# Factor tiles ahead of the activation tile, and branch outputs that start 4 to 52 bytes into longer buffers

## The chip, the cores and the metric

The kernel runs on one core of a Trainium2 chip. The metric is device time in microseconds (us); the time before is the median of two runs, 2579.45 us (2578.78 to 2580.13). Lower is better.

## The reference, cut to what matters

A two-layer decoder trunk on 256 tokens of width 2048, in float32. Each layer normalises `x`, makes one wide input projection, runs four branches on parts of it (A a state-space scan, B and D attention, C gated linear attention), projects each branch's output (width 1024) to 2048, weighs it with a sigmoid merge gate, sums the four, and applies one output projection:

```python
h = rmsnorm(x, pre_norm)
proj = h @ w_in                                   # 2048 x 20592
...                                               # out_a, out_b, out_c, out_d: (1, 256, 1024)
gates = jax.nn.sigmoid(merge.reshape(bsz, s, N_BRANCHES, D_MODEL))
mixed = (gates[:, :, 0] * (out_a @ w_branch[0]) + gates[:, :, 1] * (out_b @ w_branch[1])
         + gates[:, :, 2] * (out_c @ w_branch[2]) + gates[:, :, 3] * (out_d @ w_branch[3]))
return x + rmsnorm(mixed @ w_out, post_norm)
```

## The kernel before

All large products are computed on TensorE in the type `float32r`, each as three products of halves: an operand is split into a high half (its rounded copy) and a low half (the rest), and high x high, low x high and high x low are added up in PSUM. Two halves of everything therefore lie in SBUF:

- `hx`, in the pool `cp` (tiles that live as long as the kernel): the transposed activations of a layer, 16 blocks of 128 channels, in each block 256 tokens of the high half (`hh`) and 256 of the low half (`hl`).
- `hi` and `lo`, in the pool `st`, three buffers each: the halves of 1024 weight columns. `fetch` brings the raw weights from HBM into one of five `raw` buffers, ScalarE rounds them into `hi` (L165) and VectorE takes the difference into `lo` (L166).
- the tags `oh` and `ol` in `st`, one buffer each: the halves of whatever the next products read as activations: the normalised low-rank pair `cT`, then the branch outputs `oD`, `oC`, `oA`, `oB` one after the other, then the first half of the merged result (`m_h0`, `m_l0`). The second half of the merged result lies in slots of the pool `sl` (`m_h1`, `m_l1`). `transpose_split` fills them (L243 to L250).

A TensorE matmul has a *moving* operand, streamed from SBUF, and a *stationary* one, the weights, loaded ahead of it by a weight load (PEld in the profile). What is called weights by the model is not always what TensorE loads:

- `chunk_a` (L186 to L188) loads 128 x 128 pieces of the activations (`hx`, or the `oh`/`ol` tiles) and streams 512 columns of `hi` or `lo`. All merge gates (`acc_mA` to `acc_mD`), the branch projections (`acc_bA` to `acc_bD`), the output projection (`acc_y`) and most of the input projection go this way. One call with `hx` issues 96 matmuls (16 blocks, two token halves, three products), one call on a branch output 48.
- `chunk_b` (L203, L205, L207) loads pieces of `hi` and `lo` and streams `hx`: 512 columns (`hh` and `hl` together) with `hi`, then 256 columns (`hh`) with `lo`. `acc_g`, `acc_x`, `acc_f` go this way.
- `chunk_b4` (L228 to L230) loads pieces of `hi`/`lo` and streams 256 columns of `cT`. The `acc_small` product (L421 to L423) loads 112 columns of `hi`/`lo` and streams 256 of `hh` or `hl`.

A scheduler in the tile framework orders the instructions on each engine; the generators in `bg` (attention, scans, transposes) are stepped between weight tiles so that their small TensorE products fall between the large ones.

Tiles get their addresses in the order in which pools and tiles are made: a pool's tiles lie one behind the other, padded to 32 bytes, and a longer tile shifts all that come behind it. `cp` comes first (it ends with `hx`, `rt`, `rb`), then `st` (`raw`, `oh`, `ol`, `hi`, `lo`, `gt`), `sl` (the slots), `sm`. In each of the 128 partitions a tile starts at the same byte.

Of the kernel before, what the change touches and what calls it, by code (L numbers as in the profile page):

```python
# [9 lines left out]
F32 = mybir.dt.float32  # L10
F32R = mybir.dt.float32r
# [7 lines left out]
P = 128  # L19
T = 256  # L20
# [17 lines left out]
def trunk(ctx: ExitStack, tc: tile.TileContext, x, pos, vecs, rows, dskip, post, glaw2,  # L38
# [4 lines left out]
    cp = ctx.enter_context(tc.tile_pool(name="cp", bufs=1))  # L43
    st = ctx.enter_context(tc.tile_pool(name="st", bufs=1))
# [4 lines left out]
    def slot(i, name, dt=F32):  # L49
        return sl.tile([P, 2048], dt, tag=f"s{i}", name=name)  # L50

    def psT(name, shape=(P, 512)):
        return ps.tile(list(shape), F32, tag="t", name=name, bufs=2)
# [104 lines left out]
    def fetch(src, n=1024, own=None):  # L158
        if first_raw:
            raw = first_raw.pop(0)  # L160
        else:
            raw = st.tile([P, 1024], F32, tag="raw", name="raw", bufs=5)
            nc.sync.dma_start(raw[:, :n], src)
        hi, lo = own or (st.tile([P, 1024], F32R, tag=t, name=t, bufs=3) for t in ("hi", "lo"))
        S.copy(hi[:, :n], raw[:, :n])  # L165
        V.tensor_tensor(lo[:, :n], raw[:, :n], hi[:, :n].bitcast(F32), ALU.subtract)  # L166
        return hi, lo
# [52 lines left out]
    def chunk_b4(src, p0, nb, xh, xl, k0, name):  # L220
# [10 lines left out]
            step()  # L231
        return acc

    def transpose_split(src, nb, dh, dl, d0, scale, name):

        for b2 in range(nb // 2):
            pt = psT(f"tr_{name}{b2}").rearrange("p (a t) -> p a t", a=2)
            for j in range(2):
                for tt in range(2):
                    PE.transpose(pt[:, j, tt * P:(tt + 1) * P], src(tt, 2 * b2 + j), ident)  # L240
            d = slice(d0 + 2 * b2, d0 + 2 * b2 + 2)
            if scale is None:
                S.copy(dh[:, d], pt)  # L243
                V.tensor_tensor(dl[:, d], pt, dh[:, d].bitcast(F32), ALU.subtract)
            else:
                for j in range(2):
                    S.activation(dh[:, d0 + 2 * b2 + j], pt[:, j], AF.Copy, scale=scale(2 * b2 + j))
                for j in range(2):
                    b = 2 * b2 + j
                    V.scalar_tensor_tensor(dl[:, d0 + b], pt[:, j], scale(b), dh[:, d0 + b].bitcast(F32),  # L250
                                           ALU.mult, ALU.subtract)
            yield

    hx = cp.tile([P, 16, 2, T], F32R, tag="hx", name="hx")
    hh, hl = hx[:, :, 0], hx[:, :, 1]

    def sumsq(src, junk, acc):
        S.activation(junk, src, AF.Square, accum_out=acc)

    rt3 = cp.tile([P, 16], F32, tag="rt", name="rt")  # L260
    rt, rt2 = rt3[:, 0:2], rt3[:, 2:4]
    rb = cp.tile([P, T], F32, tag="rb", name="rb")

    def rb3(p_, n):
        return rb[p_].rearrange("p (o t) -> p o t", o=1).to_broadcast([p_.stop - p_.start, n, T])
# [120 lines left out]
    for l in range(DEPTH):  # L386
# [9 lines left out]
        cc = slot(5, "cc").rearrange("p (a b t) -> p a b t", a=2, b=2)  # L396
        cssq = small([P, 4], "cssq")
        lgate = slot(3, "lgate").rearrange("p (a b) -> p a b", a=2)
        oh = st.tile([P, 8, T], F32R, tag="oh", name="cT_h")
        ol = st.tile([P, 8, T], F32R, tag="ol", name="cT_l")  # L400
        ropej = slot(4, "qr").rearrange("p (a t) -> p a t", a=8)
        for i in range(2):
            if l == 0 and i == 1:
# [12 lines left out]
        for kh in range(2):  # L416
            hi, lo = fetch(w_sm[l, kh], 896)
# [85 lines left out]
        def cnorm_gen(l=l, cssq=cssq, cc=cc, oh=oh, ol=ol):  # L503
            r = rstd(cssq, 512, 4, "cn")
            for i in range(2):
                for tt in range(2):
                    V.tensor_scalar(cc[:, i, tt], cc[:, i, tt], r[:, 2 * i + tt:2 * i + tt + 1], None, ALU.mult)
                yield
                o = V_Q if i == 0 else V_KV
                yield from transpose_split(lambda tt, b: cc[:, i, tt, b * P:(b + 1) * P], 4, oh, ol, 4 * i,  # L510
                                           lambda b: vec[:, l, o + b:o + b + 1], f"c{i}")
# [25 lines left out]
        def mla_gen(l=l, qr=qr, qn=qn, kn=kn, dv_=dv_, lgate=lgate, oh=oh, ol=ol):  # L537
            for o, t in ((0, cos), (4, sin)):
                V.tensor_tensor(qr[:, o:o + 4], qr[:, o:o + 4],
                                t.rearrange("p (o n) -> p o n", o=1).to_broadcast([P, 4, T]), ALU.mult)  # L540
            V.tensor_tensor(qr[:, 0:4], qr[:, 0:4], qr[:, 4:8], ALU.add)
            yield

            def terms(h):
                return [(qn[:, h], kn[:, h]), (qr[:, h // 2], kr2[:, h % 2])]

            yield from attention(4, 128, 192 ** -0.5, terms, None, dv_, lgate, "D")
            noh = st.tile([P, 8, T], F32R, tag="oh", name="oD_h")
            nol = st.tile([P, 8, T], F32R, tag="ol", name="oD_l")
            res["D"] = (noh, nol)  # L550
            yield from transpose_split(lambda tt, b: lgate[:, tt, b * P:(b + 1) * P], 8, noh, nol, 0, None, "oD")

        res = {}
        mg = mla_gen()
        bg.append(mg)

# [136 lines left out]

        def finish(br, src, scale):
            def gen():
                noh = st.tile([P, 8, T], F32R, tag="oh", name=f"o{br}_h")
                nol = st.tile([P, 8, T], F32R, tag="ol", name=f"o{br}_l")
                res[br] = (noh, nol)
                yield from transpose_split(lambda tt, b: src[:, tt, b * P:(b + 1) * P], 8, noh, nol, 0, scale,
                                           "o" + br)  # L700
            g = gen()
            bg.append(g)
            return g
# [148 lines left out]
        drain()  # L852


        mh0 = st.tile([P, 8, T], F32R, tag="oh", name="m_h0")
        ml0 = st.tile([P, 8, T], F32R, tag="ol", name="m_l0")
        mh1 = slot(5, "m_h1", F32R).rearrange("p (a t) -> p a t", a=8)
        ml1 = slot(6, "m_l1", F32R).rearrange("p (a t) -> p a t", a=8)
        for half, (a_, b_) in enumerate(((mh0, ml0), (mh1, ml1))):
# [144 lines left out]
```

## Time and profile before

| | |
|---|---|
| median of the runs | 2579.45 us |
| the profiled execution | 2578.76 us |
| its span (first to last instruction) | 2577.0 us |
| TensorE (PE) busy | 2553.0 us, 99% of the span, 12666 matmuls |
| weight loads (PEld) busy | 2146.9 us, 83%, beside the matmuls |
| VectorE (DVE), ScalarE (ACT) busy | 1571.0 us (61%), 1284.7 us (50%) |
| DMA | 179 GB/s mean, the weights' queue 54.8% of the 16 engines' time |
| granted TensorE clock | 0.999 |

Matmuls are pipelined: a row's duration (some 390 ns for 512 columns) overlaps the next one's. What a matmul costs is the distance from its start to the start of the next. The tiles `oD`, `oC`, `oA`, `oB` stand in rows as `oD_h` and so on; the view leaves out numbers in names, so `m_h` is `m_h0` and `m_h1`.

### The profile page before, as it was taken

What the parts mean: (1) busy time and instruction counts of PE and PEld (TensorE: products, weight loads), DVE (VectorE), ACT (ScalarE), POOL (GpSimd) and SP (SyncE); (2) the same over time, 40 slices, a digit from 0 to 9 for tenths busy, and PEclk for the clock granted to TensorE, in tenths of its full rate; (3) what the DMA queues carried; (4) which work ended last, traced back from release to release, by engine and by line L of the source; (5) the groups of instructions that cost most, each with busy time, mean ns of one, the idle gap of its engine ahead of it and who ended that gap; (6) DMA issues with size and microseconds to landing.
All of it is one profiled execution on the core that took longest, in us unless ns stands there. A gap on an engine that the chain in (4) does not pass through costs nothing.

```text
span 2577.0 us, 32741 instructions
## 1 busy us (share of the span) xinstructions
PE 2553.0 (99%) x12666; PEld 2146.9 (83%) x12666; DVE 1571.0 (61%) x1956; ACT 1284.7 (50%) x1705; POOL 79.6 (3%) x75
## 2 busy tenths in 40 slices
PE   8999999999999999999999999999999999999998
PEld 7888888888888888888878888888888888888887
DVE  6756854776666555555566667547765665565555
ACT  6555544555445445444465455445554444444443
POOL 0000000000002000000000000000000010000000
PEclk9999999999999999999999999999999999999999
DMA  7554555555555555665655445455555655556654
GB/s 237 183 161 147 164 168 185 186 180 165 194 181 181 171 172 171 204 188 180 211 178 180 149 161 165 164 191 182 178 170 192 191 172 171 172 172 204 190 179 154
DMA packets 126571, 460.30 MB, mean 179 GB/s; under 512 B 14640, under 2 KB 15152, under 8 KB 125648
## 3 DMA queue, kind: packets, MB, share of 16 engines
q1 hardware_dynamic: 126144, 458.12, 54.8%
q8 instruction: 99, 1.62, 0.3%
q14 instruction: 56, 0.46, 0.1%
q10 hardware_dynamic: 272, 0.10, 0.0%
HBM read 453.97 MB, written 4.19 MB: 178 GB/s over the span
## 4 chain that ended last, share of the span: by engine, by line
PE 98%; ACT 1%; DVE 1%; issue 0%; DMA 0%; POOL 0%; SPq 0%; DVEq 0%; POOLq 0%; ACTq 0%
PE acc_f L203 4%; PE acc_x L203 3%; PE acc_f L205 2%; PE acc_mC L187 2%; PE acc_mA L187 2%; PE acc_mD L187 2%; PE acc_mA L186 2%; PE acc_mC L186 2%; PE acc_mA L188 2%; PE acc_mB L187 2%; PE acc_mB L186 2%; PE acc_mD L186 2%; PE acc_mC L188 2%; PE acc_mD L188 2%; PE acc_mB L188 2%; PE acc_g L203 2%
## 5 line engine op out<-in xcount | busy, mean ns | idle before, releaser
L166 DVE TENSOR_TENSOR lo<-raw,hi 128x1024 fp32r<-128x1024 f32 x842 | 1049.1, 1248 | 773.4 <-ACT hi L165 771.4
L165 ACT CAST hi<-raw 128x1024 fp32r<-128x1024 f32 x842 | 882.2, 1050 | 1035.5 <-PE acc_mB L188 95.2
L203 PE MATMUL acc_f<-hx,hi 128*128 128x512 f32 x480 | 171.5, 397 | 0.0
L205 PE MATMUL acc_f<-hx,lo 128*128 128x256 f32 x512 | 139.9, 283 | 0.0
L203 PE MATMUL acc_x<-hx,hi 128*128 128x512 f32 x360 | 128.8, 397 | 0.0
L203 PEld LDWEIGHTS acc_f<-hx,hi 128*128 128x128 f32 x480 | 90.2, 188 | 20.3
L205 PE MATMUL acc_x<-hx,lo 128*128 128x256 f32 x384 | 105.2, 284 | 0.0
L187 PE MATMUL acc_mA<-lo,hx 128*128 128x512 f32 x256 | 103.7, 405 | 0.0
L187 PE MATMUL acc_mC<-lo,hx 128*128 128x512 f32 x256 | 103.4, 404 | 0.0
L187 PE MATMUL acc_mD<-lo,hx 128*128 128x512 f32 x256 | 102.9, 402 | 0.0
L186 PE MATMUL acc_mA<-hi,hx 128*128 128x512 f32 x256 | 102.1, 399 | 0.0
L187 PE MATMUL acc_mB<-lo,hx 128*128 128x512 f32 x256 | 101.0, 395 | 0.0
L188 PE MATMUL acc_mA<-hi,hx 128*128 128x512 f32 x256 | 100.8, 394 | 0.0
L186 PE MATMUL acc_mC<-hi,hx 128*128 128x512 f32 x256 | 100.7, 393 | 0.0
L186 PE MATMUL acc_mD<-hi,hx 128*128 128x512 f32 x256 | 100.5, 392 | 0.0
L186 PE MATMUL acc_mB<-hi,hx 128*128 128x512 f32 x256 | 100.4, 392 | 0.0
L188 PE MATMUL acc_mC<-hi,hx 128*128 128x512 f32 x256 | 100.4, 392 | 0.0
L188 PE MATMUL acc_mD<-hi,hx 128*128 128x512 f32 x256 | 100.1, 391 | 0.0
L188 PE MATMUL acc_mB<-hi,hx 128*128 128x512 f32 x256 | 99.7, 390 | 0.0
L205 PEld LDWEIGHTS acc_f<-hx,lo 128*128 128x128 f32 x512 | 96.2, 188 | 2.9
L188 PE MATMUL acc_y<-hi,m_l 128*128 128x512 f32 x232 | 91.5, 394 | 0.0
L187 PE MATMUL acc_y<-lo,m_h 128*128 128x512 f32 x232 | 90.5, 390 | 0.0
(428 smaller groups left out, 5716.8 us busy)
## 6 DMA issues: line engine op xcount, KB each, us to landing
raw<-in_w_in_dram SPq DMA_DIRECT2D x624, 512.0 KB, 3.5
raw<-in_w_br_dram SPq DMA_DIRECT2D x128, 512.0 KB, 3.5
raw<-in_w_out_dram SPq DMA_DIRECT2D x64, 512.0 KB, 3.5
raw<-in_w_ukv_dram SPq DMA_DIRECT2D x16, 512.0 KB, 4.3
raw<-in_w_uq_dram SPq DMA_DIRECT2D x12, 512.0 KB, 3.8
x<-in_x_dram SPq DMA_DIRECT2D x4, 512.0 KB, 7.8
xr<-in_x_dram SPq DMA_DIRECT2D x2, 1024.0 KB, 6.8
pn<-in_post_dram SPq DMA_DIRECT2D x2, 1024.0 KB, 6.0
```

Of the source, the lines that this page charges most:

```text
L165: S.copy(hi[:, :n], raw[:, :n])
L166: V.tensor_tensor(lo[:, :n], raw[:, :n], hi[:, :n].bitcast(F32), ALU.subtract)
L186: PE.matmul(a2[tt], xh[:, k0 + k, ts_], hi[:, c], start=(k == 0), stop=False)
L187: PE.matmul(a2[tt], xh[:, k0 + k, ts_], lo[:, c], start=False, stop=False)
L188: PE.matmul(a2[tt], xl[:, k0 + k, ts_], hi[:, c], start=False, stop=(k == nk - 1))
L203: PE.matmul(acc[:, b], hi[:, c], hx[:, k].rearrange("p a t -> p (a t)"), start=(k == 0), stop=False)
L205: PE.matmul(acc[:, b, 0:T], lo[:, c], hh[:, k], start=False, stop=False)
```

## The change

Three edits, all of them to addresses:

1. `rt` (64 bytes in a partition) and `rb` (1024 bytes) are made ahead of `hx` instead of behind it.
2. The buffers of the tags `oh` and `ol` get 16 more elements (64 bytes).
3. The branch outputs start some elements into these buffers, the same number in `oh` and `ol`: D 1 and 2 (layer 0 and 1), C 5 and 4, A 9 and 12, B 13 and 3 elements of 4 bytes. `cT` and the first half of the merged result start at 0.

```diff
+    def halves(name, o=0):
+
+        h, lo = (st.tile([P, 8 * T + 16], F32R, tag=t, name=f"{name}_{t[1]}") for t in ("oh", "ol"))
+        return [a[:, o:o + 8 * T].rearrange("p (a t) -> p a t", a=8) for a in (h, lo)]
...
+    rt3 = cp.tile([P, 16], F32, tag="rt", name="rt")
+    rt, rt2 = rt3[:, 0:2], rt3[:, 2:4]
+    rb = cp.tile([P, T], F32, tag="rb", name="rb")
     hx = cp.tile([P, 16, 2, T], F32R, tag="hx", name="hx")
     hh, hl = hx[:, :, 0], hx[:, :, 1]
...
-    rt3 = cp.tile([P, 16], F32, tag="rt", name="rt")
-    rt, rt2 = rt3[:, 0:2], rt3[:, 2:4]
-    rb = cp.tile([P, T], F32, tag="rb", name="rb")
...
-        oh = st.tile([P, 8, T], F32R, tag="oh", name="cT_h")
-        ol = st.tile([P, 8, T], F32R, tag="ol", name="cT_l")
+        oh, ol = halves("cT")
...
-            noh = st.tile([P, 8, T], F32R, tag="oh", name="oD_h")
-            nol = st.tile([P, 8, T], F32R, tag="ol", name="oD_l")
+            noh, nol = halves("oD", (1, 2)[l])
...
-                noh = st.tile([P, 8, T], F32R, tag="oh", name=f"o{br}_h")
-                nol = st.tile([P, 8, T], F32R, tag="ol", name=f"o{br}_l")
+                noh, nol = halves("o" + br, {"C": (5, 4), "A": (9, 12), "B": (13, 3)}[br][l])
...
-        mh0 = st.tile([P, 8, T], F32R, tag="oh", name="m_h0")
-        ml0 = st.tile([P, 8, T], F32R, tag="ol", name="m_l0")
+        mh0, ml0 = halves("m0")
```

No instruction is added, removed or moved: on all engines the rows of the two programs agree one by one but for line numbers and the new names of two tiles (`m0_h`, `m0_l`). What differs is where operands start. The table gives the start of a tile in its partition, in bytes, and its remainder by 256, since the pieces that matmuls read are 512, 1024 or 2048 bytes apart and so keep that remainder (`acc_small` alone steps through its weights by 448 bytes):

| tile | before | mod 256 | after | mod 256 |
|---|---|---|---|---|
| `hx` | 25344 | 0 | 26432 | 64 |
| `raw`, first of five | 59200 | 64 | 59200 | 64 |
| `oh` (`cT_h`, `m_h0`) | 79680 | 64 | 79680 | 64 |
| `oh`, branch outputs | 79680 | 64 | 79684 to 79732 | 68 to 116 |
| `ol` (`cT_l`, `m_l0`) | 87872 | 64 | 87936 | 128 |
| `ol`, branch outputs | 87872 | 64 | 87940 to 87988 | 132 to 180 |
| `hi` and `lo`, first of each | 96064, 108352 | 64 | 96192, 108480 | 192 |
| slots, among them `m_h1`, `m_l1` | 157504, 182080 | 64 | 157632, 182208 | 192 |

## The prediction

> **What bounds the kernel now.** I read the page first: its head, the busy shares, the clock, and the chain that ended last.
>
> ```profile
> span 2577.0 us, 32741 instructions
> ## 1 busy us (share of the span) xinstructions
> PE 2553.0 (99%) x12666; PEld 2146.9 (83%) x12666; DVE 1571.0 (61%) x1956; ACT 1284.7 (50%) x1705; POOL 79.6 (3%) x75
> ...
> PEclk9999999999999999999999999999999999999999
> ...
> ## 4 chain that ended last, share of the span: by engine, by line
> PE 98%; ACT 1%; DVE 1%; issue 0%; DMA 0%; POOL 0%; SPq 0%; DVEq 0%; POOLq 0%; ACTq 0%
> ```
>
> TensorE is busy for 99% of the span and makes 98% of the chain, at full granted clock throughout. Then the waits of TensorE, longest first:
>
> ```profile
> engine line waited for: us in total, times, longest us
> PE tr_x L347 <- DMA x<-in_x_dram: 5.3, 1, 5.3
> PE tr_x L347 <- DVE xtot L364: 1.7, 1, 1.7
> ```
>
> The longest is the first load of `x`, and the next is 1.7 us. So no other engine's time is on the path, and a change that only moves addresses can move the end in one way: through the distance from one matmul's start to the next. I read those from the timeline, in stretches without foreign work, taking a group's first row and the first row of the group behind it.
>
> ```profile
> 1152.86 0.39 PE L186 MATMUL acc_bB<-hi,oB_h 128*128 128x512 f32 x1
> ...
> 1163.74 0.39 PE L186 MATMUL acc_mB<-hi,hx 128*128 128x512 f32 x1
> ...
> 1185.71 0.39 PE L186 MATMUL acc_bB<-hi,oB_h 128*128 128x512 f32 x1
> ```
>
> One call of `chunk_a` on a branch output is 48 matmuls: 1163.74 - 1152.86 = 10.88 us, or **226.7 ns** each. One on `hx` is 96: 1185.71 - 1163.74 = 21.97 us, or **228.9 ns** each. Shape, type, engine and source of the streamed columns are the same in both, and nothing waits. What differs is where the loaded piece starts: `oB` at 64 modulo 256 like `hi` and `lo`, `hx` at 0. I call the loaded start minus the streamed one, modulo 256, the *distance*: 0 for the branch output, -64 for `hx`. A distance of 0 is 2.2 ns cheaper at 512 columns.
>
> `chunk_b` has the roles exchanged, so its distance is +64. Here is a stretch of 31 pairs (512 columns, then 256), and beside it a group of 96 matmuls of 256 columns at distance 0, `acc_uq`:
>
> ```profile
> 729.73 0.40 PE L203 MATMUL acc_f<-hx,hi 128*128 128x512 f32 x1
> ...
> 740.67 0.40 PE L203 MATMUL acc_f<-hx,hi 128*128 128x512 f32 x1
> ...
> 113.06 0.28 PE L228 MATMUL acc_uq<-cT_h,hi 128*128 128x256 f32 x1
> ...
> 124.58 0.28 PE L228 MATMUL acc_ur<-cT_h,hi 128*128 128x256 f32 x1
> ```
>
> A pair takes (740.67 - 729.73) / 31 = **352.9 ns**, and a 256-column matmul at distance 0 takes 11.52 / 96 = **120.0 ns**. A pair at distance 0 would be 226.7 + 120.0 = 346.7 ns, so a distance of +64 costs 6.2 ns a pair. Both comparisons say the same: TensorE's pace depends on how the two operands lie to each other.
>
> **The change part by part.** No instruction comes, goes or moves, and every queue has its old order, so the sum has distances alone. By the table of addresses:
>
> - `hx` with `hi`/`lo`: `chunk_a` goes from -64 to -128, `chunk_b` from +64 to +128. In both, modulo 256, this is half a period; modulo 128 it is 0.
> - branch outputs in `chunk_a`: from 0 to -128 (high half) and -64 (low half), plus 4 to 52 bytes.
> - `cT` and the first half of the merged result: from 0 to 128 and 64 (sign by role). The second half keeps 0.
>
> The trace of before shows 0, -64 and +64 for full-sized matmuls, and so not 128, nor any distance that is no multiple of 64. Each price is therefore a choice between bounds.
>
> *hx, 5760 matmuls in `chunk_a`* (30 calls of 96 a layer, two layers). If the pattern repeats every 128 bytes, 128 is as good as 0 and they gain 2.2 ns each: -12.6 us. If it repeats every 256, the nearest rows are the two neighbours, -64 (2.2 ns over the best) and +64 (up to 6.2 over it if the whole of a pair's excess sits on one matmul): 0 to +4.0 ns each, 0 to +23 us.
>
> *hx, 1152 pairs in `chunk_b`*. The count is the 256-column rows of `acc_f`, `acc_x`, `acc_g`:
>
> ```profile
> L205 PE MATMUL acc_f<-hx,lo 128*128 128x256 f32 x512 | 139.9, 283 | 0.0
> ...
> L205 PE MATMUL acc_x<-hx,lo 128*128 128x256 f32 x384 | 105.2, 284 | 0.0
> ...
> L205 PE MATMUL acc_g<-hx,lo 128*128 128x256 f32 x256 | 70.6, 286 | 0.0
> ```
>
> With a period of 128 they gain 6.2 ns each: -7.1 us. With 256 they stay about where they are.
>
> *Branch outputs, 1536 matmuls* (four branches, two layers, four calls of 48). They are at the best distance now. A start that is 4 to 52 bytes off is shown nowhere. At worst each pays the whole excess of a pair, 6.2 ns: +9.5 us. At best the odd start frees a matmul of the part that does not scale with its columns: 226.7 - 120.0 = 106.7 ns is the price of 256 columns, which leaves 120.0 - 106.7 = 13.3 ns; without that, -20 us. I take the price of the nearest row, 2.2 ns: +3.4 us.
>
> *`cT` and the first merged half*, 576 and 384 matmuls, at the same 2.2 ns: +1.3 and +0.8 us, because their low halves land 64 off.
>
> The stores into the odd starts cost nothing that counts:
>
> ```profile
> L243 ACT CAST oB_h<-tr_oB x8: 575/586/594, 1063.3 to 2350.7; 128x512 fp32r<-128x512 f32 x8
> L244 DVE TENSOR_TENSOR oB_l<-tr_oB,oB_h x8: 678/680/684, 1064.7 to 2352.1; 128x512 fp32r<-128x512 f32 x8
> ```
>
> The 0.6 and 0.7 us stores of `oB` run beside the first merge call of B, which reads `hx` and lasts 22 us, and twice their time would still fit. Without that cover, doubled stores would cost 4 x 1.3 us a branch and layer. The split of the weights is covered too:
>
> ```profile
> L166 DVE TENSOR_TENSOR lo<-raw,hi 128x1024 fp32r<-128x1024 f32 x842 | 1049.1, 1248 | 773.4 <-ACT hi L165 771.4
> L165 ACT CAST hi<-raw 128x1024 fp32r<-128x1024 f32 x842 | 882.2, 1050 | 1035.5 <-PE acc_mB L188 95.2
> ```
>
> `raw` against `hi` goes from distance 0 to 128 there. A weight tile feeds 12 matmuls of 229 ns, 2.7 us, against 1.25 us of VectorE and 1.05 of ScalarE, which idle 773 and 1036 us before these lines, so even a tenth more would be hidden.
>
> The sum for a period of 128: -12.6 - 7.1 + 3.4 + 1.3 + 0.8 = -14.2 us, against the profiled execution's 2578.8 us: 2564.6 us. That execution is 0.7 us under the median, so I say **2565**. The bounds of the odd starts alone spread it from 2541 (all fixed parts gone) to 2571; I hold the lower end for remote.
>
> [...] A branch output's weight load lasts 188 ns and lies beside a matmul of 227:
>
> ```profile
> L186 PEld LDWEIGHTS acc_bB<-hi,oB_h x128: 187/188/188, 1086.0 to 2475.9; 128*128 128x128 f32 x128
> ```
>
> [...]
>
> **The rivals.**
>
> *The period is 256 (slower).* Then `hx` and the branch outputs all sit half a period off. [...] For it speaks the pace of `acc_small`, the only group whose distance passes through 0 and 128 (weights in steps of 448 bytes). At 0, then at 128:
>
> ```profile
> L421 PE MATMUL acc_small<-hx,hi 128*112 128x256 f32 x1 | 0.3, 276 | 0.0
> ...
> L421 PE MATMUL acc_small<-hx,hi 128*112 128x256 f32 x1 | 0.3, 282 | 0.0
> ```
>
> The matmul at 128 lasts 6 ns longer. Against it: these loads have 112 columns, every step also changes the next one's distance, and 128-column loads at distance 0 (`acc_uq`) last 283 ns, as long as the one at 128 here, so the order of prices is another one at this size. The price: `hx` half-way, 2.0 x 5760 = +11.5 us; 2496 matmuls on `oh`/`ol` half-way between 2.2 and 6.2 over the best, 4.2 x 2496 = +10.5; together +22, **2601 us**. With the upper bounds throughout, +23 and 6.2 x 2496 = +15.5, it is 2617. It decides from the point where 128 costs `hx` more than 1.2 ns over 0: then (2.2 - 1.2) x 5760 = 5.8 us of gain no longer outweigh the 5.5 us of the branch, `cT` and merged terms.
>
> *Nothing moves.* The 2.2 ns may belong to how `hh` and `hl` are interleaved, 1024 bytes apart, and not to the start: all `hx` matmuls have both. Then the first edit does nothing, and the rest gives 0 to +6 us: **2579 to 2584 us**. Then `acc_f` says against it that `hx` as the streamed operand has a loss too, where `hl` is only the second half of one stream. [...] That the change does not do what it says is excluded by the table of addresses.
>
> **How the numbers follow.** Chances: period of 128, 0.45 (2554 to 2574); nothing, 0.20 (2575 to 2584); period of 256, 0.33 (2584 to 2617); odd starts that free the fixed part, 0.02. The forecast's own range is 2556 to 2573. The range that holds 8 in 10 is 2555 to 2606: below lie about 0.04, and above it the upper third of the slower case, 0.12. A change of 2%, about what a measurement of this kernel can tell from none, would be 2528 or 2631. No case reaches either with its likely price: faster 0.02, same 0.95, slower 0.03.
>
> **What would show it.** In the profile after, `chunk_a` calls on `hx` at 21.77 us per 96 matmuls (226.7 ns) and pairs of `acc_f` at 347 ns would show the period of 128; calls at 22.1 us or more (230 ns) would show 256; 21.97 again, the interleaving. Branch calls stand at 10.88 us now: 10.99 is my price, 11.2 the upper bound, under 10.8 a gain from odd starts. The waits of TensorE should stay at 5.3 and 1.7 us. I am wrong if the time leaves the sum of these groups, that is if VectorE or ScalarE rows (1248 and 1050 ns for a weight tile) grow so far that TensorE begins to wait for `hi` or `lo`.

## The result and the profile after

The changed kernel takes 2604.82 us (two runs, 2604.12 and 2605.51) against 2579.45: a ratio of 1.010 (95% interval 1.008 to 1.012, as in the brackets below). It is slower by 25 us, where the forecast was 14 us faster. In size this is under the 2% that the forecast counted as a change; its direction is the rival's, "the period is 256", which gave 2601.

The head of the page after, its busy shares, the clock and the shares of the chain that ended last:

```profile
span 2603.7 us, 32741 instructions
PE 2580.4 (99%) x12666; PEld 2152.6 (83%) x12666; DVE 1571.9 (60%) x1956; ACT 1283.7 (49%) x1705; POOL 79.7 (3%) x75
...
PEclk9999999999999999999999999999999999999999
...
PE 98%; ACT 1%; DVE 1%; issue 0%; DMA 0%; POOL 0%; SPq 0%; DVEq 0%; POOLq 0%; ACTq 0%
```

The instructions, the clock and the chain are what they were; PE busy grew by 27.4 us and the span by 26.7. TensorE's longest waits are short as before:

```profile
PE tr_x L352 <- DMA x<-in_x_dram: 6.4, 2, 4.6
PE acc_c L186 <- ACT hi L165: 2.0, 1, 2.0
```

So the time is again in the spacing of matmuls. The timeline of the changed kernel, the first row of a branch call in layer 0, of the merge call behind it, and of the branch call after that; then the same three places in layer 1:

```profile
1130.30 0.40 PE L186 MATMUL acc_bB<-hi,oB_h 128*128 128x512 f32 x1
...
1141.60 0.39 PE L186 MATMUL acc_mB<-hi,hx 128*128 128x512 f32 x1
...
1164.00 0.40 PE L186 MATMUL acc_bB<-hi,oB_h 128*128 128x512 f32 x1
...
2424.86 0.40 PE L186 MATMUL acc_bB<-hi,oB_h 128*128 128x512 f32 x1
...
2435.85 0.39 PE L186 MATMUL acc_mB<-hi,hx 128*128 128x512 f32 x1
...
2458.16 0.39 PE L186 MATMUL acc_bB<-hi,oB_h 128*128 128x512 f32 x1
```

A call on `hx` takes 22.40 and 22.31 us, **233.3** and **232.4 ns** a matmul, against 228.9 before. That is over the 22.1 us that the prediction named as the sign of 256. The calls on `oB` take 11.30 us (235.4 ns, 13 elements in) and 10.99 us (229.0 ns, 3 elements in), against 10.88 before. The pairs of `acc_f`, 31 of them as before:

```profile
736.52 0.39 PE L203 MATMUL acc_f<-hx,hi 128*128 128x512 f32 x1
...
747.38 0.40 PE L203 MATMUL acc_f<-hx,hi 128*128 128x512 f32 x1
```

They take 350.3 ns, 2.6 less than before. The split of the weights stays covered:

```profile
L166 DVE TENSOR_TENSOR lo<-raw,hi 128x1024 fp32r<-128x1024 f32 x842 | 1049.5, 1248 | 793.0 <-ACT hi L165 789.0
L165 ACT CAST hi<-raw 128x1024 fp32r<-128x1024 f32 x842 | 880.9, 1048 | 1061.8 <-PE acc_mB L188 97.7
```

1248 ns as before and 1048 against 1050, with longer idle times ahead of them: the added time is not theirs.

From all starts in the two timelines (gaps that hold another product left out), mean ns by group, and what they make of the time:

| group | before | after | count | us |
|---|---|---|---|---|
| `chunk_a` on `hx` | 229.45 | 232.61 | 5760 | +18.2 |
| branch outputs | 227.5 | 232.4 | 1536 | +7.6 |
| merged result, first half | 227.4 | 233.0 | 384 | +2.1 |
| `cT`: 512 and 256 columns | 228.2, 120.0 | 233.2, 120.8 | 96, 480 | +0.9 |
| merged result, second half | 227.0 | 227.5 | 384 | +0.2 |
| `chunk_b` on `hx`, pairs | 352.7 | 350.7 | 1152 | -2.4 |

The sum is +26.6; the two profiled executions differ by 2605.51 - 2578.76 = 26.8 us. The second merged half, the one group that keeps distance 0, is the one that hardly moved. The pairs are at a distance of 128 now and gained a little.

### The profile page after: what moved, and what is told of

It reads as the page before. It is cut to its first block, busy times and chain, and to the rows that moved or that the text cites. A ratio compares the mean times of both kernels' runs of the same rounds, so it can differ in the third digit from the quotient of the medians.

```text
span 2603.7 us, 32741 instructions
## 1 busy us (share of the span) xinstructions
PE 2580.4 (99%) x12666; PEld 2152.6 (83%) x12666; DVE 1571.9 (60%) x1956; ACT 1283.7 (49%) x1705; POOL 79.7 (3%) x75
## 4 chain that ended last, share of the span: by engine, by line
PE 98%; ACT 1%; DVE 1%; issue 0%; DMA 0%; POOL 0%; SPq 0%; DVEq 0%; POOLq 0%; ACTq 0%
PE acc_f L203 4%; PE acc_x L203 3%; PE acc_mC L187 2%; PE acc_f L205 2%; PE acc_mA L187 2%; PE acc_mD L187 2%; PE acc_mA L188 2%; PE acc_mC L186 2%; PE acc_mB L187 2%; PE acc_mA L186 2%; PE acc_mB L188 2%; PE acc_mD L186 2%; PE acc_mB L186 2%; PE acc_mD L188 2%; PE acc_mC L188 2%; PE acc_y L188 2%
## 5 line engine op out<-in xcount | busy, mean ns | idle before, releaser
L166 DVE TENSOR_TENSOR lo<-raw,hi 128x1024 fp32r<-128x1024 f32 x842 | 1049.5, 1248 | 793.0 <-ACT hi L165 789.0
L165 ACT CAST hi<-raw 128x1024 fp32r<-128x1024 f32 x842 | 880.9, 1048 | 1061.8 <-PE acc_mB L188 97.7
```

## The experiments

### One half of the change at a time

Edit 1 alone (`rt` and `rb` ahead of `hx`, buffers and starts as before) puts everything at 64, that is at distance 0:

```diff
-        oh, ol = halves("cT")
+        oh = st.tile([P, 8, T], F32R, tag="oh", name="cT_h")
+        ol = st.tile([P, 8, T], F32R, tag="ol", name="cT_l")
```

and so for the branch outputs and the merged result.

> Edit 1 alone: the factor tiles ahead of hx, branch buffers as before. All operands of the large products then start at 64 modulo 256. Theory R (the price is set by the distance between the loaded and the streamed start, modulo 256): hx calls of chunk_a go from 228.9 to 226.7 ns a matmul, pairs of chunk_b from 352.9 to about 346.7 ns, branch calls stay at 226.7; 5760 x 2.2 + 1152 x 6.2 = 20 us less, 2559 us. Rival I (the interleaving of hh and hl makes hx dear, not its start): 2579 us, 228.9 ns as before. Rival M (the first edit itself is what costs): slower than 2579 us.

Measured: **2570.92 us**, ratio 0.997 [0.996, 0.998]. This part of the change is faster than before, by 7.8 us, where 20 were expected. Its timeline at the place shown above:

```profile
1115.79 0.39 PE L186 MATMUL acc_bB<-hi,oB_h 128*128 128x512 f32 x1
...
1126.67 0.39 PE L186 MATMUL acc_mB<-hi,hx 128*128 128x512 f32 x1
...
1148.43 0.39 PE L186 MATMUL acc_bB<-hi,oB_h 128*128 128x512 f32 x1
```

The call on `hx` now takes 21.76 us, 226.7 ns, like one on a branch output. So the 2.2 ns of before belonged to the start of `hx` and not to its interleaved halves, and "nothing moves" is refuted. The gain on `hx` is smaller than 2.2 x 5760 = 12.7 us because the stretches that small float32 products interrupt don't reach 226.7 at once. In the same kernel, the first matmul behind such a product, the ninth after it and the ninth after that:

```profile
836.73 0.39 PE L187 MATMUL acc_fv<-lo,hx 128*128 128x512 f32 x1
...
838.81 0.39 PE L187 MATMUL acc_fv<-lo,hx 128*128 128x512 f32 x1
...
840.85 0.39 PE L187 MATMUL acc_fv<-lo,hx 128*128 128x512 f32 x1
```

The first nine take 2.08 us (231 ns each), the next nine 2.04 (226.7). The kernel has 86 such stretches of twenty or more matmuls, and by the starts in the trace each is back at 226.7 within ten. Over all calls on `hx` the mean is 228.24, against 229.45 before: 7.0 us. The pairs were to give 7.1 and give 1.8 (351.2 ns against 352.7): at distance 0 they do not come down to the 346.7 that the prediction put together from two other groups, so most of its 6.2 ns was no matter of distance. The two gains make 8.8 us by these means, 1.0 more than the times differ.

Edits 2 and 3 alone leave `hx` at 0, while `hi` and `lo` go to 192, so its distance is +64:

```diff
-    rt3 = cp.tile([P, 16], F32, tag="rt", name="rt")
...
     hx = cp.tile([P, 16, 2, T], F32R, tag="hx", name="hx")
...
+    rt3 = cp.tile([P, 16], F32, tag="rt", name="rt")
```

> Edits 2 and 3 alone: hx stays at 0 modulo 256, hi and lo go to 192, branch outputs as in the change. Distance of hx in chunk_a becomes +64, in chunk_b -64. Theory R: branch calls at about 232.5 ns as in the change (1536 x 5.8 = +9 us), the first merged half and cT +3 us; hx at +64 is new: between the price of -64 (no change, so 2591 us in all) and that of 128 (+3.7 x 5760 = +21 us, 2612 us). Pairs of chunk_b at -64: 346 to 353 ns, 0 to -8 us. Rival O (the odd starts make the whole loss): 2604 us with hx calls at 228.9 ns.

Measured: **2608.3 us**, ratio 1.012 [1.010, 1.013].

```profile
1143.50 0.39 PE L186 MATMUL acc_mB<-hi,hx 128*128 128x512 f32 x1
...
1165.90 0.40 PE L186 MATMUL acc_bB<-hi,oB_h 128*128 128x512 f32 x1
```

A call on `hx` at +64 takes 22.40 us, 233.3 ns; at -64 it took 228.9. With a period of 128 these two distances would be one and the same. This row by itself excludes it for `chunk_a`.

### The change without the odd starts

```diff
-        return [a[:, o:o + 8 * T].rearrange("p (a t) -> p a t", a=8) for a in (h, lo)]
+        return [a[:, 0:8 * T].rearrange("p (a t) -> p a t", a=8) for a in (h, lo)]
```

> The change with all branch outputs at element 0 of the longer buffers. Theory R: hx and its distance of 128 are as in the change (232.6 ns), the branch calls sit at 128 (high half) and -64 (low half) without the odd bytes, which should be worth less than 2 ns a matmul: 1536 x 2 = 3 us, so 2602 to 2608 us. Rival O (the odd starts make the loss): back to 2579 us.

Measured: **2605.17 us**, ratio 1.010 [1.009, 1.012], as the change itself. All branch groups now have means of 232.6 to 233.1 ns, where the odd starts gave 228.9 to 235.5. So an offset of 4 to 52 bytes moves a branch by -4 to +3 ns and the eight of them cancel; what cost the branches their 5 ns is the 64 bytes that each buffer grew by (with the old buffers, in edit 1 alone, their groups have 226.7 to 228.2).

### Everything shifted by 128

Edit 1 with an unused tile of 128 bytes in front of all others, so that every remainder changes and no distance does:

```diff
+    cp.tile([P, 32], F32, tag="shift", name="shift")
```

> Edit 1 with an unused 128-byte tile ahead of everything: all starts move by 128, all distances stay 0. Theory R: as edit 1 alone, 2559 us, within 1 us. Rival A (what counts is a start's own remainder, with 64 as the good one): hx calls over 228 ns, 2579 us or more.

Measured: **2570.56 us**, ratio 0.997 [0.996, 0.998], the same as edit 1. At distance 0, then, moving both operands by 128 bytes changes nothing: how they lie to each other counts, not where they lie.

### hx alone at a distance of 128

Edit 1 with the 128 bytes of the tile `id2` made behind `hx` in place of ahead of it. The small tiles made between the two places move with `hx`; the branch outputs, `hi` and `lo` stay:

```diff
-    id2 = cp.tile([P, 32], F32R, tag="id2", name="id2")
     lvl = cp.tile([P, 8, P], U8, tag="lvl", name="lvl")
...
+    id2 = cp.tile([P, 32], F32R, tag="id2", name="id2")
```

> The first edit, and the identity tile id2 made behind hx in place of ahead of it, so that hx alone starts 128 bytes further and everything else keeps distance 0 or 128 (the pairs, hx against the activation's counterpart, too). The theory that the distance on hx carries most of the loss: 2570.9 + 5760 x (232.6 - 228.2 ns) = 2596, with hx calls of about 22.3 us. The rival that the branch outputs' starts and the merged product carry it: 2571, with hx calls of 21.8 us.

Measured: **2595.25 us**, ratio 1.006 [1.004, 1.008].

```profile
1127.33 0.40 PE L185 MATMUL acc_bB<-hi,oB_h 128*128 128x512 f32 x1
...
1138.27 0.40 PE L185 MATMUL acc_mB<-hi,hx 128*128 128x512 f32 x1
...
1160.58 0.40 PE L185 MATMUL acc_bB<-hi,oB_h 128*128 128x512 f32 x1
```

The calls on `hx` take 22.31 us (232.4 ns) and those on the branch outputs stay at 10.9. From edit 1, 128 bytes cost 24.3 us. The small products, which also read some of the moved tiles, take 176 us in both kernels, and the pairs of `chunk_b` 350.7 ns against 351.2, so the loss is in `chunk_a` on `hx`. Its mean is 232.6 ns, as in the change, against 229.45 before: that is about the +18.2 of the table, and the term that the forecast had at -12.6.

### Small distances

Everything at distance 0, and the branch outputs at offsets around it, in one buffer for both halves (D keeps its 1 and 2; `rt` has 8 columns, which gives the room):

```diff
-        h, lo = (st.tile([P, 8 * T + 16], F32R, tag=t, name=f"{name}_{t[1]}") for t in ("oh", "ol"))
+        both = st.tile([P, 16 * T + 64], F32R, tag="ohl", name=name)[:, o:o + 16 * T].rearrange("p (h a t) -> p h a t", h=2, a=8)
...
-                noh, nol = halves("o" + br, {"C": (5, 4), "A": (9, 12), "B": (13, 3)}[br][l])
+                noh, nol = halves("o" + br, {"C": (4, 8), "A": (12, 60), "B": (56, 63)}[br][l])
```

> Everything starts at the same remainder of 256 bytes (distance 0 for hx, the activation tile and the merged product), and the branch outputs start at o floats in one buffer for both halves: layer 0 / layer 1 at a distance of 4 / 8 bytes (D), 16 / 32 (C), 48 / 240 (A), 224 / 252 (B). The two small tiles and the buffers differ in size from the change, no work is left out. Theory G (starts count in steps of 64 bytes, so that anything within 64 bytes of distance 0 costs 226.7 ns): the branch groups stay at 226.7 and the time is that of the first edit alone, 2571. Theory E (only equal starts are cheap; any other distance costs the 229 to 235.5 ns that the change showed): branch groups at 229 to 235, time 2571 + 1536 x (2 to 9 ns) = 2574 to 2585. Theory C (a curve: the price rises with the distance): 4 and 252 bytes nearest to 226.7, 48 and 224 nearest to 232; about 2576.

Measured: **2575.95 us**, ratio 0.999 [0.998, 1.000]. The calls of D in layer 0 (+4 bytes) and of B in layer 0 (224) and layer 1 (252):

```profile
414.16 0.39 PE L186 MATMUL acc_bD<-hi,oD 128*128 128x512 f32 x1
...
425.32 0.40 PE L186 MATMUL acc_mD<-hi,hx 128*128 128x512 f32 x1
...
1117.40 0.39 PE L186 MATMUL acc_bB<-hi,oB 128*128 128x512 f32 x1
...
1128.59 0.39 PE L186 MATMUL acc_mB<-hi,hx 128*128 128x512 f32 x1
...
2396.05 0.39 PE L186 MATMUL acc_bB<-hi,oB 128*128 128x512 f32 x1
...
2406.93 0.39 PE L186 MATMUL acc_mB<-hi,hx 128*128 128x512 f32 x1
```

They take 11.16, 11.19 and 10.88 us: 232.5, 233.1 and 226.7 ns. Theory G falls, since 4 bytes cost as much as 128. C and E both have the time, but C falls as a curve: in uninterrupted stretches +4 takes 232.4, +8 230.7, +16 226.7, +32, +48 and 224 233.2, and 240 and 252 226.7. E lacks the cheap 16, 240 and 252. The next runs put one of these on all of `hx`.

### hx four bytes after and four bytes before

Edit 1 with a longer buffer for `hx`; o is 1, then 63:

```diff
-    hx = cp.tile([P, 16, 2, T], F32R, tag="hx", name="hx")
+    hx = cp.tile([P, 16 * 2 * T + 64], F32R, tag="hx", name="hx")[:, o:o + 32 * T].rearrange("p (k h t) -> p k h t", k=16, h=2)
```

> The first edit, with hx one float into a longer buffer: its distance to hi and lo is +4 bytes, all other large products stay at 0. The price seen on a branch output at +4 (232.4 ns against 227.3 for the same group at 0) carried over to 5760 matmuls: 2571 + 5760 x 5.0 ns = 2600, hx calls of 22.3 us. Rival (what counts is how far apart, so that 4 bytes cost next to nothing over this many matmuls): 2571 to 2575, calls of 21.8 us.

> The same with hx 63 floats into its buffer: its distance is 252, that is 4 bytes ahead of 0. The price of the branch output at 252 (226.7 ns, as at 0): 2571, hx calls of 21.8 us. Rival (any start that is not the same costs, the branch group at 252 was an accident of its small sample): 2596 to 2600, calls of 22.3 us.

Measured: **2603.1 us** (1.009 [1.007, 1.011]) and **2593.87 us** (1.006 [1.004, 1.007]). The first is near the 2600 that the price foretold, but in part by luck. The call on `hx`, at +4:

```profile
1141.71 0.39 PE L186 MATMUL acc_mB<-hi,hx 128*128 128x512 f32 x1
...
1164.01 0.39 PE L186 MATMUL acc_bB<-hi,oB_h 128*128 128x512 f32 x1
```

22.30 us, as expected. But over all its calls `hx` has a mean of 232.38 ns against 228.24, which is 24 us and not the 29 of the price; another 8.6 us are the pairs of `chunk_b`, 358.6 ns against 351.2, which the expectation had left out. The second isn't what the branch group at 252 had foretold, 2571. Its timeline shows two paces at one distance: 120 matmuls of `acc_lg`, which follow the small products of `acc_small`, and the merge call behind a branch call.

```profile
67.41 0.40 PE L186 MATMUL acc_lg<-hi,hx 128*128 128x512 f32 x1
...
95.41 0.40 PE L186 MATMUL acc_lg<-hi,hx 128*128 128x512 f32 x1
...
1138.59 0.39 PE L186 MATMUL acc_mB<-hi,hx 128*128 128x512 f32 x1
...
1160.35 0.39 PE L186 MATMUL acc_bB<-hi,oB_h 128*128 128x512 f32 x1
```

28.00 us / 120 = 233.3 ns, and 21.76 / 96 = **226.7 ns**, with the same operands at the same distance of 252. The cheap stretch comes straight behind a branch call at distance 0. The trace has this throughout: wherever a merge call follows a branch call at 0 directly, it runs at 226.7 until a small product cuts in. In the merge call before the one shown, transposes (`tr_m`) do:

```profile
1104.67 0.39 PE L186 MATMUL acc_mB<-hi,hx 128*128 128x512 f32 x1
...
1112.83 0.39 PE L186 MATMUL acc_mB<-hi,hx 128*128 128x512 f32 x1
1113.07 0.71 PE L240 MATMUL tr_m<-ident,mixed 128*128 128x128 f32 x5
...
1114.08 0.40 PE L186 MATMUL acc_mB<-hi,hx 128*128 128x512 f32 x1
...
1116.18 0.40 PE L186 MATMUL acc_mB<-hi,hx 128*128 128x512 f32 x1
```

Ahead of them 36 matmuls take 8.16 us (226.7 ns each), behind them 9 take 2.10 (233.3). Of the 86 stretches that came back to 226.7 at distance 0, none does at 252.

### Everything at 252

To see whether the pace is carried over from the products ahead, I also put `cT`, the branch outputs and the first merged half 4 bytes ahead of `hi` and `lo` (one buffer for both halves, 56 elements longer; `hx` 7 elements into a buffer 8 longer, with `rt` and `rb` behind it):

```diff
+        both = st.tile([P, 16 * T + 56], F32R, tag="ohl", name=name)[:, 55:55 + 16 * T].rearrange("p (h a t) -> p h a t", h=2, a=8)
...
+    hx = cp.tile([P, 16 * 2 * T + 8], F32R, tag="hx", name="hx")[:, 7:7 + 32 * T].rearrange("p (k h t) -> p k h t", k=16, h=2)
```

> Everything that is loaded from hx and from the buffers of the branch outputs starts 4 bytes ahead of hi and lo (distance 252), so that no large product but the second half of the output projection has distance 0. In the run with hx alone at 252, calls on hx took 22.4 us, but 21.76 behind a branch call at distance 0. If the pace at 252 has two steady patterns and a call goes on in the one that the products ahead of it were in: no call ahead is at 0 now, so the calls on hx behind a branch call take 22.4 us (233.3 ns), the branch calls 11.2, and the time is 2594 + 785 x 6.6 (the cheap seventh of the hx matmuls) + 1536 x 6 + 960 x 5 ns = 2613. If the place in the program decides: those calls stay at 21.76, and the time is 2594 + 9 + 5 = 2608. If a branch output at 252 is cheap whatever came ahead (as one was in the run with offsets around 0): branch calls of 10.9, 2594 to 2599.

Measured: **2606.57 us**, ratio 1.011 [1.009, 1.012].

```profile
1130.85 0.40 PE L186 MATMUL acc_bB<-hi,oB 128*128 128x512 f32 x1
...
1142.05 0.40 PE L186 MATMUL acc_mB<-hi,hx 128*128 128x512 f32 x1
...
1164.45 0.40 PE L186 MATMUL acc_bB<-hi,oB 128*128 128x512 f32 x1
```

Both calls are at 233.3 ns now (11.20 and 22.40 us), in both layers. So neither the place in the program nor the offset by itself made them cheap: at 252 there are two steady paces. The one of the products ahead is carried on, and without a product at distance 0 ahead none of the branch and merge calls got into the cheap one. The time is 6 us under the 2613 of the sum, which had charged `cT` and the merged half in full: the 256-column products of `cT` take 117.7 ns here, less than the 119.9 at distance 0, and the first merged half 228.2.

### Half the weight load

Does the length of the weight load take part in the loss? Here the second and third product of `chunk_a` on `hx`, in all but the last block of a call, load 64 columns in place of 128, so that the kernel leaves out the low-half terms of half the tokens. This is done at distance 0 (on edit 1) and with `hx` alone at 128:

```diff
-                PE.matmul(a2[tt], xh[:, k0 + k, ts_], lo[:, c], start=False, stop=False)
-                PE.matmul(a2[tt], xl[:, k0 + k, ts_], hi[:, c], start=False, stop=(k == nk - 1))
+                m_ = 64 if xh is hh and k < nk - 1 else P
+                ts_ = slice(tt * P, tt * P + m_)
+                PE.matmul(a2[tt][0:m_], xh[:, k0 + k, ts_], lo[:, c], start=False, stop=False)
+                PE.matmul(a2[tt][0:m_], xl[:, k0 + k, ts_], hi[:, c], start=False, stop=(k == nk - 1))
```

> The first edit alone, but in chunk_a on hx the second and third product of each block (the last block excepted) load 64 columns of hx in place of 128, so that the low-half terms of half the tokens are left out. Streamed columns and the count of matmuls are unchanged. Base for the next run. If the pace at distance 0 is set by streaming alone: 2571 as before. If the fixed 13.3 ns of a matmul hang on the length of its load: about 2571 - 3600 x 6.7 ns = 2547.

> The same half loads with hx alone at a distance of 128. With full loads the step from 0 to 128 cost 24.3 us. If the loss is the load of 128 columns meeting the stream, in proportion to the load's length, two of three loads halved leave two thirds: h1 - h0 = 16 us. If it is a loss per matmul whatever the load's length (a matter of starts): 24 us. If only long loads collide: 8 us or less.

Measured: **2572.95 us** (0.998 [0.997, 0.999]) and **2578.46 us** (0.999 [0.999, 1.000]). The merge call at distance 0, then at 128, and the loads of one line of the second kernel (shortest, median and longest in ns, then by shape):

```profile
1126.86 0.39 PE L186 MATMUL acc_mB<-hi,hx 128*128 128x512 f32 x1
...
1148.89 0.39 PE L186 MATMUL acc_bB<-hi,oB_h 128*128 128x512 f32 x1
```

```profile
1129.44 0.40 PE L185 MATMUL acc_mB<-hi,hx 128*128 128x512 f32 x1
...
1151.48 0.40 PE L185 MATMUL acc_bB<-hi,oB_h 128*128 128x512 f32 x1
```

```profile
L188 PEld LDWEIGHTS acc_mB<-lo,hx x256: 133/134/188, 1061.5 to 2463.1; 128*64 128x64 f32 x120, 128*128 128x128 f32 x8
```

The step from 0 to 128 shrinks from 24.3 to 5.5 us, and in the call shown it is gone: 22.03 and 22.04 us, 229.5 ns both. A loss that is a matter of starts alone would have stayed at 24, one in proportion to the load's length at 16; the size is that of the third case, 8 us or less. So the length of the load takes part. That only long loads collide is not shown, since the kernel that the step starts from has changed too: at distance 0 the call with half loads runs at 229.5 ns and not 226.7. The call that mixes loads of 188 and 134 ns thus costs 2.8 ns a matmul of its own, which may hide part of the other loss. (The time rose by only 2 us because some 110 matmuls behind small products are 263 ns from the next, where such gaps were 337 ns with full loads.) The steady pace did not fall with shorter loads (229.5 ns against 226.7), so nothing here ties the fixed part of a matmul to the length of its load.

## Why the prediction was wrong

**Right: what bounds it.** TensorE's spacing is the whole of the time; the table's sum, +26.6 of 26.8, leaves nothing for another engine, and the covers that the sum relied on held.

**Right: that the distance counts.** Edit 1 alone and its shifted copy agree (2570.9 and 2570.6), and `hx` at distance 0 has the 226.7 ns that the prediction read off the branch outputs.

**The step that failed: the period.** The prediction took 128 to be as good as 0 for `hx` and wrote -12.6 us. For `chunk_a` the period is not 128; 128 costs 232.4 to 233.3 ns, nearly the dearest seen, and the term was +18.2. For -64 and +64, one and the same modulo 128, I had read 2.2 ns a matmul and 6.2 ns a pair, in exchanged roles. That looks like a row against the period, but it is not one: in edit 1 alone a pair at distance 0 takes 351.2, so +64 costs it 1.5 ns and not 6.2. No full-sized row of before had a distance of 128, and the sign of the largest term hung on it. The run with edits 2 and 3 alone decides, with `hx` in one role at both: 228.9 at -64 and 233.3 at +64.

**The other terms.** The first two have the same cause, the third another:

- Branch outputs: +3.4 forecast, +7.6 measured. The price of -64 was the nearest row but the lowest of the dear distances. The upper bound, 6.2 x 1536 = 9.5, held; no odd start freed a fixed part (no branch group is under 228.9 ns).
- `cT` and first merged half: +2.1 forecast, +3.0 measured.
- Pairs of `chunk_b`: -7.1 forecast, -2.4 measured. Here 128 is as good as 0, as forecast: 350.7 ns at 128, in the change and with `hx` alone moved, and 351.2 at 0. What failed is the reference: pairs at 0 do not have the 346.7 that I made of two groups with equal loads and columns.

**The rivals.** "The period is 256" had the direction, the point from which it decides (128 had to cost more than 1.2 ns over 0; it costs 5.7 to 6.6 in uninterrupted calls) and nearly the time: 2601 against 2604.8, within its own 2584 to 2617 and in the range given. Half-way values were too low for `hx` (+11.5 against +18.2) and right for all of `oh` and `ol` (+10.5 against +10.6); the pairs' -2.4 it left out. That the period of `chunk_a` is 256, and not 512 or more, is shown at distance 0 by the run with small distances. `hx` starts 69888 bytes ahead of `hi` in that run, an odd multiple of 256, and in edit 1 alone 69632, an even one:

```profile
1128.59 0.39 PE L186 MATMUL acc_mB<-hi,hx 128*128 128x512 f32 x1
...
1150.36 0.39 PE L186 MATMUL acc_bB<-hi,oB 128*128 128x512 f32 x1
```

21.77 us there, 21.76 in edit 1 alone. For the pairs, where 0 and 128 cost the same (351.2 and 350.7 ns), a period of 256 is not shown. I had given this rival 0.33.

**The weight load and the odd starts.** 128 bytes between the loaded and the streamed start of `hx` cost 24.3 us with full loads and 5.5 with halved ones: the load's length takes part, and more than that is not shown. Taking the odd starts out changed nothing (2605.17 against 2604.82). With them the eight branch groups have means of 228.9 to 235.5 ns, C and A of layer 1 (16 and 48 bytes in) 232.6 and 230.8.

## What to carry to other kernels

Where TensorE is the bound and every matmul reloads its weights, write down where the loaded and the streamed operand start, modulo 256, and put them at the same remainder: here that is worth 7.8 us against the kernel before and 34 against the change, with no instruction moved. Where matmuls of 512 and of 256 columns take turns, as in `chunk_b`, 128 bytes off cost nothing here, but 4 bytes could (358.6 ns a pair). A small tile, or 64 bytes on a buffer, shifts all that is made behind it, so the table of starts belongs beside every change of a buffer's size. And when the sign of a forecast hangs on a distance that no row shows, move one tile to that distance and run it first: here 128 bytes of one tile settled it. A price read against a sum of two other groups is not a measured price, as the 346.7 ns of a pair showed.

## What the runs showed of the hardware

- Matmuls of 128 x 128 on 512 columns of `float32r`, with a weight load for each, start 226.7 ns apart when both operands start at the same remainder of 256 bytes, 228.9 with the loaded one at -64, and 232.4 to 233.3 with it at +64 and 128. Four bytes after are enough for 232.4. These are uninterrupted calls of `chunk_a`.
- Pairs of 512 and 256 columns (`chunk_b`) follow another order, by their means over a kernel: 351.2 ns at 0, 350.7 at 128, 352.7 at +64, 351.7 at -64, and 358.6 with the streamed tile four bytes after.
- The pace is not a function of the distance alone. At 252 the same call ran at 226.7 behind a product at distance 0, until a small product cut in, and at 233.3 from there on. At 0 it came back to 226.7 by itself within ten matmuls of a small product. So 252, and perhaps 16 and 240, which were seen only behind calls at 0, are cheap only in company.
- What in the memory or in TensorE's sequence makes these patterns is open; the runs show that the length of the weight load takes part (a step of 24.3 us with full loads, 5.5 with halved ones).
